# Four transposes in each feed-forward of a diffusion-transformer step: between two blocks of products instead of inside one

## The chip, the core and the metric

The kernel runs on one core of one Trainium2 chip. The metric is the device time of one launch in microseconds (us). Times of instructions below are in us, or in nanoseconds (ns) where marked so.

## What is computed

The reference is one inference step of a two-layer backbone. 128 context tokens and 128 latent tokens pass through the same weights, so every product has 256 columns of tokens. A layer is a mixer (latent and grouped-query attention in layer 0, differential attention in layer 1) and then a gated feed-forward. Each of these has a shift, a scale and a gate, six vectors of 2048 values per layer that come from a condition through `w_ada`.

```
mod = silu(cond) @ w_ada[l] + b_ada[l]             # sh1, sc1, gt1, sh2, sc2, gt2
h = rmsnorm(x, g_norm_mix[l]) * (1 + sc1) + sh1
x = x + gt1 * mixer(h)
h = rmsnorm(x, g_norm_ffn[l]) * (1 + sc2) + sh2
u = h @ w_up                                       # 2048 -> 2 * 5632
u = conv3(u) + b_conv                              # over positions, each feature by itself
x = x + gt2 * ((silu(gate) * val) @ w_down)        # 5632 -> 2048
```

## The kernel before

**Products.** Everything is float32. Each operand is split into a rounded high part and the remainder: a weight chunk becomes `wh` (by ScalarE, L237) and `wl` (by VectorE, L238), an activation becomes a high half and a low half of `hx`. `gemm` (L323) adds up one chunk of 128 output features in one PSUM bank `acc`. A block is 128 rows of the contraction, and it takes three products: `wh` by the high half, `wh` by the low half, `wl` by the high half. In the trace and in the order these read wh, wh, wl. A chunk of the up-projection has 16 blocks, 48 products, and a chunk of the down-projection has 22 blocks, 66 products. Every product is a load of 128x128 weights (PEld in the profile) and a matmul with 256 columns. 1024 columns, 8 blocks, make one tile of `wh` or `wl`, so that block 8 of an up chunk is the first of its second tile.

**The feed-forward.** `ffn` (L1246) runs once per layer. It takes half of the 88 chunks of `w_up`, two for each of the 22 features of a half, then the down-projection's 16 chunks over that half, and then both again (`NQ` is 2). The first three chunks arrive already multiplied (`ready`), since `modulated` (L666) starts them before the norm is known. The others go through `product`, which calls `gemm`.

**Sums of `w_ada`.** The vectors of `mod` are computed in units of 512 values. A unit's sums stand in a PSUM bank with the features along the free axis; ScalarE copies them to the tile `am`, TensorE transposes `am` in four pieces of 128x128 into the PSUM bank `misc` (`turn` in `ada_finish`, L411, with ident from the constants `cst`), and VectorE reduces these to `mod` (L424) and adds the bias (L426). One such unit, the first quarter of the feed-forward's gate, begins in `modulated`; its last step, the four transposes, is handed to `ffn` as the list `turn`.

**Order of the work.** A scheduler orders each engine's instructions, except those that `keep_order` has pinned. `ffn` pins the order of the first products that it computes itself: the list `in_order` holds what goes with each of them, nothing with two, `turn` with the third, nothing with the fourth. A callable `between` is called by `gemm` in block 8 behind the first of the block's three products (L334 to L336), so that the transposes stand between the two products that use the same `wh`. All three product kinds of these chunks and the transposes are pinned in this order.

Of the kernel before, what the change touches and what calls it, by code (L numbers as in the profile page):

```python
# [21 lines left out]
NT = 2 * T  # L22
# [66 lines left out]
def step_kernel(ctx: ExitStack, tc: tile.TileContext, A: dict):  # L89
# [4 lines left out]
    def keep_order(i):  # L94
        if not any(i is j for j in kept):
            kept[:] = [i]
            tc.keep_in_program_order(i)
# [28 lines left out]
    def banks(name):  # L126
        return tc.tile_pool(name=name, bufs=1, space=PSUM)
# [7 lines left out]
    def T_(pl, shape, tag, dt=F32, bufs=None):  # L135
        kw = {} if bufs is None else {"bufs": bufs}
        return pl.tile(shape, dt, tag=tag, name=nm(tag), **kw)
# [98 lines left out]
    def split(out_hi, out_lo, src, pin=lambda i: i):  # L236
        pin(act.copy(out_hi, src))  # L237
        pin(dve.tensor_tensor(out=out_lo, in0=src, in1=out_hi.bitcast(F32), op=ALU.subtract))  # L238
# [81 lines left out]
            pin(pe.matmul(ps[c][:, :NT], wl, xh(k), start=False, stop=b))  # L320
        return [p[:, :NT] for p in ps]

    def gemm(blocks, xh, xl, n=NT, first=0, between=None):  # L323

        fixed = lambda i: keep_order(i) if between is not None else i
        ps = T_(pacc, [P, 512], "acc")
        last = len(blocks) - 1
        for i in range(last + 1):  # L330
            k = (i + first) % (last + 1)
            wh, wl = blocks[k]
            fixed(pe.matmul(ps[:, :n], wh, xh(k), start=(i == 0), stop=False))
            if callable(between):  # L334
                if i == (last + 1) // 2:
                    between()  # L336
            elif between and i in between:
                between[i]()
            fixed(pe.matmul(ps[:, :n], wh, xl(k), start=False, stop=False))
            fixed(pe.matmul(ps[:, :n], wl, xh(k), start=False, stop=(i == last)))  # L340
        return ps[:, :n]


# [94 lines left out]
    def load_row():  # L438
        feat["row"] = T_(feat["home"], [P, 2, D], "condb")
        sp.dma_start(out=feat["row"], in_=A["condb"])  # L440
        for r in range(2):
            keep_order(act.activation(feat["row"][:, r], feat["row"][:, r], AF.Silu))
# [118 lines left out]
    def pump(rows, feats=0.0, until=None):  # L561

        until = until or RLIMIT[stage[0]]
        step()
        side_pump()
        ada["due"] += rows
        while ada["due"] >= 0.25:
            if ada["i"] >= until and not later:
                ada["due"] = 0.0
                break  # L570
            ada["due"] -= 0.25 if ada["i"] >= until else 0.25 * ada["pew"]
            row_step(until)
        feat["due"] += feats
        while feat["due"] >= 1.0 and feat["i"] < FLIMIT[stage[0]]:
            feat["due"] -= 1.0
            feature_step()
# [44 lines left out]
    def raw_rows(u, l, which):  # L621

        at = [0]

        def row(c):
            for g in range(2):
                s = slice(g * T, (g + 1) * T)
                act.activation(u[:, c, s], x[:, c, s], AF.Identity, scale=scl[:, l, which, c, g:g + 1])  # L630
            for g in range(2):
                s = slice(g * T, (g + 1) * T)
                dve.scalar_tensor_tensor(out=u[:, c, UW + g * T:UW + (g + 1) * T], in0=x[:, c, s],
                                         scalar=scl[:, l, which, c, g:g + 1],
                                         in1=u[:, c, s].bitcast(F32), op0=ALU.mult, op1=ALU.subtract)

        def behind(c):
            for _ in range(2 if c < KD - 1 else KD):
                if at[0] > c:
                    break  # L640
                if c == KD - 1:
                    ensure(l, 3 * which + 1)
                elif (l, 3 * which + 1, at[0] // 4) not in done:
                    break
                row(at[0])
                at[0] += 1

        return behind
# [14 lines left out]
    def raw_tile(pl, tag):  # L663
        return home(pl, tag)[:, :KD * 2 * UW].rearrange("p (k n) -> p k n", k=KD)
# [580 lines left out]

    def ffn(hx, W, ready, turn, l, st):  # L1246
        xh, xl = (lambda k: hx[:, k, :NT]), (lambda k: hx[:, k, NT:2 * NT])
        product = lambda: ready.pop(0) if ready else gemm(W.chunk(), xh, xl, between=in_order.pop(0) if in_order else None)
        WD = Weights(A["w_down"][l], KQ, TB)
        cw = ada["cw"]  # L1250
        with tc.tile_pool(name=f"ffn{l}", bufs=1) as fp, banks(f"pffn{l}") as pf:
            feat["home"], feat["pool"] = fp, pf
            feat["due"] = 0.0
            in_order = [{}, {}] + turn + [{}]
            T_(fp, [P, SHIFT // 4], "pad")

            def conv(m):
                early = bool(ready)
                pin = keep_order if early else lambda i: i
                ps = product()  # L1260
                y = T_(fp, [P, NT], "cv", bufs=3)
                pin(act.activation(y, ps, AF.Identity, scale=cw[:, 1, m:m + 1], bias=cw[:, 3, m:m + 1]))  # L1262
                y3 = y.rearrange("p (g t) -> p g t", g=2)
                p3 = ps.rearrange("p (g t) -> p g t", g=2)
                pin(dve.scalar_tensor_tensor(out=y3[:, :, 1:], in0=p3[:, :, :T - 1],  # L1265
                                             scalar=cw[:, 0, m:m + 1], in1=y3[:, :, 1:],
                                             op0=ALU.mult, op1=ALU.add))
                pin(dve.scalar_tensor_tensor(out=y3[:, :, :T - 1], in0=p3[:, :, 1:],  # L1268
                                             scalar=cw[:, 2, m:m + 1], in1=y3[:, :, :T - 1],
                                             op0=ALU.mult, op1=ALU.add))  # L1270
                if early and ready:
                    W.ahead(pin)
                return y

            def up(q):
                gs = []
                for i in range(q * KQ, (q + 1) * KQ):
                    rate = 0 if i < LATE else FRATE["up"]
                    fine[0] = False
                    gate = conv(i)  # L1280
                    pump(0, rate)
                    val = conv(NFF + i)
                    pump(0, rate)
                    act.activation(gate, gate, AF.Silu)
                    dve.tensor_tensor(out=val, in0=gate, in1=val, op=ALU.mult)
                    g = T_(fp, [P, ROW], "g", F32R, bufs=KQ)
                    split(g[:, :NT], g[:, NT:2 * NT], val)
                    gs.append(g)
                    if i == LATE - 1:
                        load_row()  # L1290
                return gs

            def down(gs, q):
                u, rows = None, None
                if q == NQ - 1 and l < NL - 1:
                    u = raw_tile(keep, "hx")
                    rows = raw_rows(u, l + 1, 0)
                for c in range(KD):
                    quiet = q == NQ - 1 and c >= KD - QUIET[0]
                    fine[0] = quiet  # L1300
                    if q == 0:
                        ensure(l, 5, [c // 4])
                    ps = gemm(WD.chunk(), lambda k: gs[k][:, :NT], lambda k: gs[k][:, NT:2 * NT])
                    if l == NL - 1 and q == NQ - 1 and c == KD - 1:
                        last_residual(ps, l, 1, c, st)
                    else:
                        residual(ps, l, 1, c, st if q == NQ - 1 else None)
                    if rows:
                        rows(c)
                    if l == NL - 1 and q == NQ - 1 and c in EARLY:  # L1310
                        act.activation(x[:, c], x[:, c], AF.Identity, scale=C("gfin")[:, c:c + 1])
                    pump(0, 0 if quiet else FRATE["down"])
                return u

            for q in range(NQ):
                gs = up(q)
                u = down(gs, q)
            while feat["i"] < FLIMIT[stage[0]]:
                feature_step()
            return u  # L1320


    with banks("pab") as ppool["ada"]:
# [3 lines left out]
        first = {1: load_half(1, 0, "araw"), 0: load_half(0, 0, "raw")}  # L1327
# [8 lines left out]
        with tc.tile_pool(name="beside", bufs=1) as beside:  # L1336
            o = mixer_ab(hx, rb0, beside)
            with tc.tile_pool(name="raw", bufs=1) as rp:
# [3 lines left out]
                W = Weights(A["w_up"][0], KD, 1)  # L1342
# [5 lines left out]
    with tc.tile_pool(name="cc", bufs=1) as cp, banks("pc") as ppool["ada"]:  # L1348
# [3 lines left out]
        W = Weights(A["w_in_c"], KD, 1)  # L1352
# [5 lines left out]
        W = Weights(A["w_up"][1], KD, 1)  # L1358
# [149 lines left out]
```

## Time and profile before

| | |
|---|---|
| time, median of 3 runs | 2363.69 us (2362.99 to 2365.67) |
| the profiled execution's own time | 2362.23 us |
| its span, first to last instruction | 2360.4 us |
| TensorE busy, and loading weights | 98% and 94% of the span |
| VectorE, ScalarE, GpSimdE busy | 78%, 50%, 7% |
| mean granted TensorE clock | 0.995 |
| read from HBM | 605.12 MB, 258 GB/s over the span |

The profile gives each engine's busy time, the span in 40 slices, and the chain of work that ended last. A busy TensorE says only that matmuls are in flight: the ends of its matmuls are modelled. How fast it works is read from the number of matmuls in a stretch of time, or from the length of an uninterrupted piece of the chain and its count.

### The profile page before, as it was taken

The numbers are of one execution on the slowest core, as the hardware profiler recorded it, in microseconds if no ns is written. First come the engines' busy times: TensorE is split into PE (matmuls) and PEld (weight loads), VectorE is DVE, ScalarE is ACT, GpSimd is POOL, SyncE is SP. The second block draws the span as 40 slices with busy tenths as digits, with TensorE's granted clock in tenths as the row PEclk, the third lists the DMA queues.
The fourth block names the chain that finished last, engine by engine and source line by source line (L and its number), as shares of the span: only waits on it lengthen the run. The fifth ranks groups of instructions, "written<-read, shape, count | busy, mean of one in ns | idle before, by whom it ended". The sixth has DMA issues, their size and how long they took to land.

```text
span 2360.4 us, 47894 instructions
## 1 busy us (share of the span) xinstructions
PE 2323.6 (98%) x19666; PEld 2214.8 (94%) x19666; DVE 1850.4 (78%) x2864; ACT 1191.4 (50%) x1980; POOL 176.7 (7%) x242
## 2 busy tenths in 40 slices
PE   6999999999999999999999999999999999999998
PEld 4788778999999999999999999999999999999998
DVE  3569767889989999999988888787998655666644
ACT  4246545665554455555564545557555434555443
POOL 0002101300000000001130000122000000000011
PEclk9999999999999999999999999999999999999999
DMA  9988888677777777677778888667666555555553
GB/s 362 352 327 300 305 321 325 239 281 265 267 259 283 295 271 267 251 263 273 281 279 304 302 293 315 233 249 274 251 250 242 183 193 181 193 181 190 185 185 119
DMA packets 106811, 612.97 MB, mean 260 GB/s; under 512 B 11552, under 2 KB 19552, under 8 KB 38880
## 3 DMA queue, kind: packets, MB, share of 16 engines
q1 hardware_dynamic: 106592, 609.92, 70.8%
q8 instruction: 154, 2.52, 0.4%
q14 instruction: 65, 0.53, 0.1%
HBM read 605.12 MB, written 4.75 MB: 258 GB/s over the span
## 4 chain that ended last, share of the span: by engine, by line
PE 96%; DVE 2%; DMA 1%; ACT 1%; issue 0%; SPq 0%; POOL 0%; DVEq 0%; ACTq 0%
PE acc L104 88%; PE ada L104 4%; PE att L104 2%; PE att L107 1%; PE misc L104 1%; DVE wl L238 1%; DMA araw<-w_ada 0%; PE ada L107 0%; ACT wh L237 0%; DMA raw<-w_in_ab 0%; DVE x L1370 0%; DVE aacc L481 0%; DVE nt L604 0%; DMA block<-w_ada 0%; DVE proj L960 0%
## 5 line engine op out<-in xcount | busy, mean ns | idle before, releaser
L104 PE MATMUL acc<-hx,wh 128*128 128x256 f32 (+1 forms) x7296 | 1280.3, 280 | 5.5 <-ACT hx L614 4.3
L237 ACT CAST wh<-raw 128x1024 fp32r<-128x1024 f32 (+2 forms) x824 | 794.5, 976 | 955.8 <-PE acc L104 760.1
L238 DVE TENSOR_TENSOR wl<-raw,wh 128x1024 fp32r<-128x1024 f32 (+2 forms) x824 | 920.2, 1132 | 309.6 <-ACT wh L237 307.0
L104 PEld LDWEIGHTS acc<-hx,wh 128*128 128x128 f32 x7296 | 1114.0, 189 | 37.9 <-issue 17.2
L104 PE MATMUL acc<-hx,wl 128*128 128x256 f32 (+1 forms) x3648 | 1016.7, 279 | 4.4 <-DVE wl L238 4.4
L104 PEld LDWEIGHTS acc<-hx,wl 128*128 128x128 f32 x3648 | 686.9, 188 | 5.5 <-DVE wl L238 5.5
L104 PE MATMUL acc<-g,wh 128*128 128x256 f32 x2816 | 488.2, 278 | 0.0
L104 PEld LDWEIGHTS acc<-g,wh 128*128 128x128 f32 x2816 | 429.2, 189 | 0.0
L104 PE MATMUL acc<-g,wl 128*128 128x256 f32 x1408 | 391.7, 278 | 0.0
L104 PE MATMUL acc<-hxc,wh 128*128 128x256 f32 (+1 forms) x1536 | 276.6, 281 | 0.0
L452 DVE CUSTOM_DVE_ANT_0 junk<-araw,condb 128x2048 f32<-128x2048 f32 x120 | 275.8, 2299 | 0.0
L104 PEld LDWEIGHTS acc<-g,wl 128*128 128x128 f32 x1408 | 264.2, 188 | 0.0
L104 PEld LDWEIGHTS acc<-hxc,wh 128*128 128x128 f32 x1536 | 235.9, 188 | 8.7 <-issue 8.4
L104 PE MATMUL acc<-hxc,wl 128*128 128x256 f32 (+1 forms) x768 | 213.5, 278 | 0.0
L200 POOL TENSOR_TENSOR sqacc<-sqacc,sq 128x256 f32<-128x256 f32 x62 | 71.1, 1146 | 1539.9 <-ACT sq L196 1533.3
L481 DVE SCALAR_TENSOR_TENSOR aacc<-block,condw,aacc 128x512 f32<-128x512 f32 x240 | 172.1, 755 | 12.4 <-DMA block<-w_ada 12.3
L104 PEld LDWEIGHTS acc<-hxc,wl 128*128 128x128 f32 x768 | 144.5, 188 | 0.3
L104 PE MATMUL ada<-araw,condw 128*32 128x512 f32 (+1 forms) x736 | 91.3, 591 | 12.8 <-DMA araw<-w_ada 12.8
L1262 ACT ACTIVATE cv<-acc,convw 128x256 f32<-128x256 f32 x170 | 95.0, 559 | 0.0
L773 DVE SCALAR_TENSOR_TENSOR x<-acc,mod,x 128x128 f32<-128x128 f32 x190 | 57.4, 344 | 39.7 <-PE acc L104 39.6
L1268 DVE SCALAR_TENSOR_TENSOR cv<-acc,convw,cv 128x254 f32<-128x254 f32 x170 | 81.4, 479 | 3.3
L1265 DVE SCALAR_TENSOR_TENSOR cv<-acc,convw,cv 128x254 f32<-128x254 f32 x170 | 80.8, 475 | 0.0
(229 smaller groups left out, 1400.4 us busy)
## 6 DMA issues: line engine op xcount, KB each, us to landing
raw<-w_up SPq DMA_DIRECT2D x176, 1024.0 KB, 4.8
araw<-w_ada SPq DMA_DIRECT2D x146, 1024.0 KB, 6.0
raw<-w_down SPq DMA_DIRECT2D x88, 1024.0 KB, 4.8
raw<-w_in_c SPq DMA_DIRECT2D x48, 1024.0 KB, 6.9
block<-w_ada SPq DMA_DIRECT2D x128, 256.0 KB, 5.4
raw<-w_in_ab SPq DMA_DIRECT2D x19, 1024.0 KB, 7.1
raw<-w_out_ab SPq DMA_DIRECT2D x16, 1024.0 KB, 7.0
raw<-w_out_c SPq DMA_DIRECT2D x16, 1024.0 KB, 5.8
```

The source lines that it names most:

```text
L104: return self.placed(nc.tensor.matmul(*a, **kw))
L107: return self.placed(nc.tensor.transpose(*a, **kw))
L200: eng.tensor_tensor(out=st["acc"], in0=st["acc"], in1=sq, op=ALU.add)
L237: pin(act.copy(out_hi, src))
L238: pin(dve.tensor_tensor(out=out_lo, in0=src, in1=out_hi.bitcast(F32), op=ALU.subtract))
L452: keep_order(dve.tensor_tensor_reduce(out=T_(feat["pool"], [P, D], "junk"), in1=feat["row"][:, c], in0=feat["raw"].rearrange("p g n -> p ( ...
L481: i = dve.scalar_tensor_tensor(out=acc[c], in0=block, scalar=condw[:, k, c:c + 1], in1=acc[c], op0=ALU.mult, op1=ALU.add)
L773: dve.scalar_tensor_tensor(out=x[:, c, s], in0=ps[:, s], scalar=mod[:, l, 3 * which + 2, c, g:g + 1], in1=x[:, c, s], op0=ALU.mult, op1=AL ...
L1262: pin(act.activation(y, ps, AF.Identity, scale=cw[:, 1, m:m + 1], bias=cw[:, 3, m:m + 1]))
L1265: pin(dve.scalar_tensor_tensor(out=y3[:, :, 1:], in0=p3[:, :, :T - 1], scalar=cw[:, 0, m:m + 1], in1=y3[:, :, 1:], op0=ALU.mult, op1=ALU.add))
L1268: pin(dve.scalar_tensor_tensor(out=y3[:, :, :T - 1], in0=p3[:, :, 1:], scalar=cw[:, 2, m:m + 1], in1=y3[:, :, :T - 1], op0=ALU.mult, op1=A ...
```

## The change

`gemm` gets a second hook, `behind`, which is called in the same block 8, but after the block's third product. `ffn` hands the unit's transposes to it in place of `between`. The chunks that are pinned are the same as before.

```
-    def gemm(blocks, xh, xl, n=NT, first=0, between=None):
+    def gemm(blocks, xh, xl, n=NT, first=0, between=None, behind=None):
...
-        fixed = lambda i: keep_order(i) if between is not None else i
+        fixed = lambda i: keep_order(i) if between is not None or behind else i
...
             fixed(pe.matmul(ps[:, :n], wh, xl(k), start=False, stop=False))
             fixed(pe.matmul(ps[:, :n], wl, xh(k), start=False, stop=(i == last)))
+            if behind and i == (last + 1) // 2:
+                behind()
         return ps[:, :n]
...
-        product = lambda: ready.pop(0) if ready else gemm(W.chunk(), xh, xl, between=in_order.pop(0) if in_order else None)
+        product = lambda: ready.pop(0) if ready else gemm(W.chunk(), xh, xl, **(in_order.pop(0) if in_order else {}))
...
-            in_order = [{}, {}] + turn + [{}]
+            in_order = [dict(between={})] * 2 + [dict(behind=t) for t in turn] + [dict(between={})]
```

What this does to the order of TensorE's instructions in layer 0's feed-forward, third chunk of those that it computes itself (`acc_5782` is the chunk's bank, `wh_5778` and `wl_5779` the weight tiles of blocks 8 to 15, `am_5605` the unit's sums; a line with - stands in the kernel before, one with + in the changed one):

```order
 L104 MATMUL acc_5782<-hx_5443,wh_5774 128x256 x2
 L104 MATMUL acc_5782<-hx_5443,wl_5775 128x256
-L104 MATMUL acc_5782<-hx_5443,wh_5778 128x256
-L107 MATMUL misc_5808<-cst_74,am_5605 128x128 x4
-L104 MATMUL acc_5782<-hx_5443,wh_5778 128x256
+L104 MATMUL acc_5782<-hx_5443,wh_5778 128x256 x2
 L104 MATMUL acc_5782<-hx_5443,wl_5779 128x256
+L107 MATMUL misc_5810<-cst_74,am_5605 128x128 x4
 L104 MATMUL acc_5782<-hx_5443,wh_5778 128x256 x2
 L104 MATMUL acc_5782<-hx_5443,wl_5779 128x256
```

The four transposes moved two products later, from between the two products with the same `wh` to between the `wl` product of block 8 and the first `wh` product of block 9. The same in layer 1's feed-forward:

```order
 L104 MATMUL acc_20251<-hx_19913,wh_20243 128x256 x2
 L104 MATMUL acc_20251<-hx_19913,wl_20244 128x256
-L104 MATMUL acc_20251<-hx_19913,wh_20247 128x256
-L107 MATMUL misc_20277<-cst_74,am_20075 128x128 x4
-L104 MATMUL acc_20251<-hx_19913,wh_20247 128x256
+L104 MATMUL acc_20251<-hx_19913,wh_20247 128x256 x2
 L104 MATMUL acc_20251<-hx_19913,wl_20248 128x256
+L107 MATMUL misc_20279<-cst_74,am_20075 128x128 x4
 L104 MATMUL acc_20251<-hx_19913,wh_20247 128x256 x2
 L104 MATMUL acc_20251<-hx_19913,wl_20248 128x256
```

The same move happened there. VectorE, ScalarE, GpSimdE and the DMA queue keep their instructions in the same order, and TensorE has no other place that differs; only line numbers behind `gemm` are two higher.

## The prediction

> **What bounds the kernel now.** I read the page first.
>
> ```profile
> PE 2323.6 (98%) x19666; PEld 2214.8 (94%) x19666; DVE 1850.4 (78%) x2864; ACT 1191.4 (50%) x1980; POOL 176.7 (7%) x242
> ...
> PE 96%; DVE 2%; DMA 1%; ACT 1%; issue 0%; SPq 0%; POOL 0%; DVEq 0%; ACTq 0%
> ```
>
> TensorE (PE) is busy for 98% of the span and makes up 96% of the chain that ended last. So an edit pays only if it changes the number of TensorE's instructions, a wait of TensorE, or the pace at which it takes its instructions. The number is the same here. Next I read the chain in order of time, at the two places where the edited transposes stand (misc, L107).
>
> ```profile
> 487.59 0.44 PE misc L107 x4
> 488.02 690.34 PE acc L104 x6090
> ...
> 1632.12 0.43 PE misc L107 x4
> 1632.56 715.04 PE acc L104 x6071
> ```
>
> Behind each of them there is a single piece of chain with no wait inside it: nearly all of the feed-forward of that layer. The first needs 690.34 / 6090 = 113.36 ns per product, the second 715.04 / 6071 = 117.78 ns. The products have the same shape and the same code. The difference is 4.42 ns per product, and over 6071 products it is 26.9 us, 1.1% of the kernel. That is the only thing at these places that is large, so I looked for what it hangs on, with the stages' table.
>
> ```profile
> core 0: us, PE busy (x) PEld busy (x) DVE busy (x) ACT busy (x) POOL busy (x), PEclk, DMA share, GB/s
> 500.00:1170.00 670.00, 670.00 (x5914) 670.00 (x5913) 624.61 (x802) 340.00 (x468) 16.40 (x13) 1.00 0.73 269
> 1640.00:2340.00 700.00, 700.00 (x5945) 700.00 (x5945) 470.19 (x618) 334.77 (x443) 15.77 (x13) 1.00 0.56 199
> ```
>
> The slower stage is layer 1 (700 / 5945 = 117.7 ns against 670 / 5914 = 113.3). It isn't slower by the clock: the granted clock (PEclk) is 1.00 in both. It isn't slower by load elsewhere: there VectorE (470 of 700 us), the DMA share (0.56) and the traffic (199 GB/s) are all lower than in layer 0. So TensorE has two rhythms for the same stream, and keeps the one it has fallen into for 6000 products. The question is what it falls into behind the transposes. The timeline of TensorE around them, first in layer 0, then the end of the same piece in layer 1:
>
> ```profile
> 487.31 0.28 PE L104 MATMUL acc<-hx,wh 128*128 128x256 f32 x1
> 487.42 0.60 PE L107 MATMUL misc<-cst,am 128*128 128x128 f32 x4
> 487.78 0.36 PE L104 MATMUL acc<-hx,wh 128*128 128x256 f32 x1
> 487.98 0.28 PE L104 MATMUL acc<-hx,wl 128*128 128x256 f32 x1
> 488.10 0.40 PE L104 MATMUL acc<-hx,wh 128*128 128x256 f32 x2
> 488.34 0.28 PE L104 MATMUL acc<-hx,wl 128*128 128x256 f32 x1
> 488.46 0.39 PE L104 MATMUL acc<-hx,wh 128*128 128x256 f32 x2
> ...
> 1632.63 0.40 PE L104 MATMUL acc<-hx,wh 128*128 128x256 f32 x2
> 1632.87 0.28 PE L104 MATMUL acc<-hx,wl 128*128 128x256 f32 x1
> 1632.99 0.40 PE L104 MATMUL acc<-hx,wh 128*128 128x256 f32 x2
> ```
>
> From one wl to the next is 0.36 us at 487.98, while a block in the fast rhythm takes 3 x 113.3 = 340 ns. So behind the transposes layer 0 too starts slowly, and is back to 0.39 for a pair of wh at 488.46; in layer 1 the pair stays at 0.40. The choice falls within the first two or three blocks behind the break, and no one asks again until the mixer or the end.
>
> **The change part by part.**
>
> *The break itself.* In layer 0 it is the time from 487.31 to 488.10, 0.79 us for three products and four transposes. Three products alone are 0.34 us, so the break costs 0.45 us. The nearest break of the new kind, four transposes of a unit's `am` behind a wl and ahead of a wh, stands in the mixer of layer 0:
>
> ```profile
> 416.80 0.28 PE L104 MATMUL acc<-hx,wl 128*128 128x256 f32 x1
> 416.92 0.60 PE L107 MATMUL ada<-cst,am 128*128 128x128 f32 x4
> 417.27 0.48 PE L104 MATMUL acc<-hx,wh 128*128 128x256 f32 x2
> 417.60 0.28 PE L104 MATMUL acc<-hx,wl 128*128 128x256 f32 x1
> 417.71 0.39 PE L104 MATMUL acc<-hx,wh 128*128 128x256 f32 x2
> ```
>
> From 416.80 to 417.71 is 0.91 us for four products (0.453 alone) and the transposes: 0.46 us. The change of the break's own cost is +0.01 us, and the rows' rounding puts it between -0.02 and +0.03. Twice that is nothing.
>
> *The transposes come 0.23 us later* (two products). The reader of `misc` is VectorE's reduction:
>
> ```profile
> 489.39 0.19 DVE L424 TENSOR_REDUCE mod<-misc 128x8 f32<-128x32 f32 x1
> ...
> 1633.92 0.18 DVE L424 TENSOR_REDUCE mod<-misc 128x8 f32<-128x32 f32 x1
> ```
>
> It starts 1.37 us behind the end of the transposes in the chain (488.02) and 1.37 behind 1632.55, held by VectorE's earlier work. So 0.23 us is hidden, with 1.1 us to spare; without that cover it would cost VectorE 0.23 us, and TensorE nothing as long as its weights are ahead. No other engine's order, no wait and no DMA moves, as the order shows. The wait for `wl` of block 8 now ends before the transposes instead of behind them. That takes away 0.45 us of cover from it, but TensorE showed no gap there.
>
> *The rhythm behind the break.* This is the term that matters. The trace before has breaks of both kinds, and the chain shows the pace of what follows each. First those where a unit's transposes of `am` stand between two blocks, the new place; the first, one near the middle, and the last:
>
> ```profile
> 37.76 0.22 PE ada L107 x2
> 37.98 7.07 PE acc L104 x60
> ...
> 417.08 0.44 PE ada L107 x4
> 417.52 21.77 PE acc L104 x192
> ...
> 1545.26 0.44 PE ada L107 x4
> 1545.70 32.66 PE acc L104 x288
> ```
>
> 32.66 / 288 = 113.4 ns and 21.77 / 192 = 113.4 are fast; 7.07 / 60 = 117.8 is slow. From the first to the last of these there are eight with 18 products or more behind them: the first, with two transposes, is slow, the other seven, with four, are fast. Now the old place, inside a block. There are five in which the unit's transposes come last, from 488.02 (fast) to 1632.56 (slow), and the three between these are like the first of them:
>
> ```profile
> 1219.91 0.44 PE ada L107 x4
> 1220.34 11.31 PE acc L104 x96
> ```
>
> 11.31 / 96 = 117.8 ns. So four of five were slow inside a block, and one of eight between blocks. The feed-forward of layer 0 is the lucky one of the five. Other short work doesn't keep to that, in either place:
>
> ```profile
> 220.19 0.44 PE misc L104 x4
> 220.64 2.12 PE acc L104 x18
> ...
> 1259.29 0.44 PE att L107 x4
> 1259.73 10.90 PE acc L104 x96
> ```
>
> The first four are spreads of a norm's factor between two blocks, and slow (2.12 / 18 = 117.8); the second four are transposes of another tile inside a block, and fast (10.90 / 96 = 113.5). So the place alone doesn't settle it.
>
> I take it that layer 1 goes to the fast rhythm and layer 0 stays in it. Layer 1 then gains 6071 x 4.42 ns = 26.9 us, layer 0 nothing. The bounds of this term are -26.9 us (layer 1 becomes fast) and +26.9 us (layer 0 becomes slow: 6090 x 4.42). I take the first, since it is nearest to the seven breaks that share the operation, the count and the place. Whether faster products then meet a wait is answered by layer 0: it ran at 113.36 ns without one, with VectorE at 624.61 of 670 us and 269 GB/s, more than layer 1 will ask for.
>
> [...]
>
> *The mixer of layer 1* lies between the two feed-forwards, from 1178 to 1632 us, with many breaks of its own. Its instructions and order are the same. All of it from one rhythm to the other would be 454 x 4.42 / 117.78 = 17 us, but each break chooses anew, so I allow ±2 us and take 0.
>
> *Sum.* Against the profiled execution: 2362.23 - 26.9 = 2335.3 us. It was 1.5 us below the median of the runs, 2363.69, from which the same sum gives 2336.8. I forecast 2336.0.
>
> **The rivals.**
>
> *Layer 1 falls into the slow rhythm again.* For it: the three blocks ahead of the break are the same, and the spreads of a norm between blocks were slow. Against it: seven of eight. Price 0: 2362.2 by the profile, 2363.7 by the median. [...]
>
> *The two layers change places*, layer 0 slow and layer 1 fast: -26.9 + 26.9, again about 2363. Layer 0's one break inside a block was fast, so its redraw can lose.
>
> *Slower: layer 0 loses the fast rhythm, and layer 1 doesn't find it.* The place is the piece from 488.02 on. The price is 6090 x 4.42 = 26.9 us: 2389 by the profile, 2390.6 by the median. It decides if the pair of wh at the third block behind the break still shows 0.40 instead of 0.39 us. For it: layer 0's present state is the exception among the five, so a new draw has something to lose there, and the first break between blocks was slow. Against it: it needs two slow outcomes where seven of eight were fast.
>
> That the change does not do what it says is excluded by the order, which shows the move in both layers.
>
> **How the numbers follow.** Seven of eight for each layer would give 0.77 for both fast. Three of these seven are followed by at most 24 products, and the slow spreads share the place, so I take less: 0.70 for the forecast, 0.18 for layer 1 slow again, 0.04 for the exchange, 0.08 for slower. The likeliest case's own range is 2332 to 2340: the two sums, ±2 for the mixer, and about ±2 for the spread of runs (2362.99 to 2365.67). It holds only 0.70, so the range must take in the two cases without a change, up to 2366: 2332 to 2366, which leaves out 0.08. A measurement of this kernel can tell about 0.2% (4.7 us) from no change. Faster 0.70, same 0.18 + 0.04 = 0.22, slower 0.08.
>
> **What would show it.** In the chain of the changed kernel the piece behind layer 1's transposes has 6069 products: 688 us confirms the forecast, 715 refutes it. The piece behind layer 0's has 6088: 690 us confirms, 717 refutes. The time per product should be 113.4 ns in both at a granted clock of 1.00, with no wait of TensorE between. The break should cost 0.45 us as before, and the reduction at L424 should start no later relative to the end of the transposes. I am wrong if the time falls with a pace that hasn't changed, or if the pace changes in the middle of a piece, without a break.

## The result, and the profile after

| | median, us | runs | ratio to the kernel before (95% interval) |
|---|---|---|---|
| before | 2363.49 (2362.08 to 2367.36) | 12 | |
| changed | 2364.68 (2357.75 to 2369.18) | 12 | 1.0002 (0.9991 to 1.0012) |

The change made no difference that can be measured. The forecast of 2336.0 us was wrong; the rival in which layer 1 falls into the slow rhythm again came true. The profiled execution took 2364.03 us, with a span of 2362.2.

The chain of waits of the changed kernel, at the transposes of layer 0 and of layer 1 (start, length, what, number of instructions):

```profile
487.97 0.44 PE misc L107 x4
488.41 690.11 PE acc L104 x6088
...
1633.65 0.43 PE misc L107 x4
1634.08 714.81 PE acc L104 x6069
```

The pieces have the 6088 and 6069 products that the move implies, and their paces are those of before: 690.11 / 6088 = 113.36 ns and 714.81 / 6069 = 117.78 ns. The stages' table has the same numbers of matmuls as before, 5914 and 5945, at a clock of 1.00:

```profile
500.00:1170.00 670.00, 670.00 (x5914) 670.00 (x5914) 624.38 (x802) 340.24 (x468) 16.44 (x13) 1.00 0.73 269
1640.00:2340.00 700.00, 700.00 (x5945) 700.00 (x5945) 470.84 (x618) 335.15 (x444) 15.71 (x13) 1.00 0.56 199
```

The timeline around layer 1's transposes shows the break in its new place:

```profile
1633.37 0.28 PE L104 MATMUL acc<-hx,wl 128*128 128x256 f32 x1
1633.49 0.60 PE L107 MATMUL misc<-cst,am 128*128 128x128 f32 x4
1633.84 0.48 PE L104 MATMUL acc<-hx,wh 128*128 128x256 f32 x2
1634.16 0.28 PE L104 MATMUL acc<-hx,wl 128*128 128x256 f32 x1
1634.28 0.40 PE L104 MATMUL acc<-hx,wh 128*128 128x256 f32 x2
```

From 1633.37 to 1634.28 it is 0.91 us for four products and the transposes, as forecast. Little was lost elsewhere. The mixer of layer 1 took 1.1 us longer, inside the 2 us that the prediction allowed: TensorE waited there for a transfer of `w_ada` in the middle of a unit's sums, and the 129 products behind these, from 1198.59 us on, ran at 117.7 ns by their starts, where the kernel before ran them at 113.3. The expected gain simply never began.

The starts in the trace are kept to 1 ns, though the rows round them to 10. "By the starts" below means by these unrounded ones. By them the first transpose begins 115 ns behind the last product's start in layer 0 and 119 ns in layer 1, in the kernel before and in the changed one; this distance is called the first gap. So the two streams arrive at the transposes in different states, though both at 113.3 ns a product, and the change left both states as they were. The first gap became the lead for the experiments.

### The profile page after: what moved, and what is told of

The parts are those of the page before. It is cut to its first block, busy times and chain, and to the rows that moved or that the text cites. A ratio compares the mean times of both kernels' runs of the same rounds, so it can differ in the third digit from the quotient of the medians.

```text
span 2362.2 us, 47894 instructions
## 1 busy us (share of the span) xinstructions
PE 2322.5 (98%) x19666; PEld 2213.5 (94%) x19666; DVE 1850.1 (78%) x2864; ACT 1191.6 (50%) x1980; POOL 177.0 (7%) x242
## 4 chain that ended last, share of the span: by engine, by line
PE 95%; DVE 2%; DMA 2%; ACT 0%; issue 0%; POOL 0%; DVEq 0%; SPq 0%; ACTq 0%
PE acc L104 87%; PE ada L104 4%; PE att L104 2%; DMA araw<-w_ada 1%; PE att L107 1%; PE misc L104 1%; DVE wl L238 1%; DMA raw<-w_in_ab 0%; PE ada L107 0%; DMA x<-xT 0%; DVE sqacc L200 0%; DVE aacc L483 0%; DVE x L1372 0%; ACT wh L237 0%; DVE nt L606 0%
```

## The experiments

Theory A: the pace behind a break is fixed by the state in which the stream arrives and by the number of transposes, and the place has no part in it. Theory B, that of the prediction: the place loads a draw. Theory C: layer 1's stream is slow by itself.

Each kernel was compared with the kernel before in runs on the same chip. There it took 2365.03 us (median of 13 runs), 2364.02 (13) and 2365.01 (7) in the three sittings.

### One transpose more, in layer 1

```
-            for b in range(2 if on_dve else 4):
+            for b in [0, 1, 2, 3, 3] if l and pin is keep_order else range(2 if on_dve else 4):
```

> A fifth transpose (the fourth once more, to the same place) stands behind the four in layer 1, and nothing else differs from the changed kernel. Theory A, what follows a break is fixed by the state in which the stream arrives and by the instructions of the break, not by its place: the break is 0.11 us longer, so its outcome may change: about 2364 us + 0.1 if layer 1 stays at 117.8 ns a product, 2337 us if it goes to 113.4. Theory B, the place decides by a loaded draw: fast in most cases, 2337 us. Theory C, layer 1's stream settles at 117.8 ns by itself, whatever the break: 2364 us, and no break can change it.

Measured: 2336.8 us, ratio 0.9875 (0.9856 to 0.9893). The chain of this kernel at layer 1:

```profile
1636.83 0.55 PE misc L107 x5
1637.38 687.86 PE acc L104 x6069
```

687.86 / 6069 = 113.34 ns. A redundant instruction of 0.11 us saved 28 us, about the 26.9 that the prediction had priced. Theory C falls, and so does any doubt about the price. VectorE and the DMA kept up, as layer 0 had suggested.

### The same four in the first chunk, in both layers

```
-            in_order = [dict(between={})] * 2 + [dict(behind=t) for t in turn] + [dict(between={})]
+            in_order = [dict(behind=t) for t in turn] + [dict(between={})] * 3
```

> The same four transposes, behind block 8 of the first chunk that the feed-forward computes itself in place of the third, in both layers: 96 products earlier in the same stream. Theory A: the stream arrives in the same state, so layer 0 stays fast, layer 1 slow, 2364 us. Theory B: a new draw, 2337 us in most cases. Theory C: 2364 us.

Measured: 2364.4 us, ratio 0.9988 (0.9963 to 1.0014). Nine of ten runs lay between 2363.0 and 2368.3 us, and one, the profiled one, took 2336.55. In that one the chain shows layer 1 fast:

```profile
1618.42 4.33 PE acc L104 x35
1622.75 0.44 PE misc L107 x4
...
1623.19 698.74 PE acc L104 x6165
```

698.74 / 6165 = 113.34 ns. Here only 35 products lie between the last sums of the unit and the transposes, where the changed kernel has 131, and by the starts this stream arrived slow. So near another break the arriving state can differ from run to run. The nine others have no trace; that they arrived fast is inferred from their times. The run doesn't tell A from B by itself.

### Many breaks

Every third chunk of the up-projection got a break (transposes between products) of 1, 2, 3, 4, 5, 6, 8 and again 1, 2, ... transposes of `am`, 27 in each layer. In the first kernel they lie between two blocks in layer 0 and inside a block in layer 1; in the second the places are exchanged (`l == 0`).

```
+    def more(n):
+        pt = bank()
+        for b in range(n):
+            keep_order(pe.transpose(pt[:, b % 4 * P:(b % 4 + 1) * P], last_am[0][:, b % 4 * P:(b % 4 + 1) * P], ident))
...
+            for n in (1, 2, 3, 4, 5, 6, 8) * 4:
+                in_order += [dict(between={})] * 2 + [dict(extra=(l == 1, n))]
```

> Beside the unit's transposes, every third chunk of the up-projection gets a break of 1, 2, 3, 4, 5, 6 or 8 further transposes of the same tile into the free bank, whose results nobody reads: between two blocks in layer 0, inside a block (behind its first product) in layer 1; about 26 breaks in each layer, 110 transposes, 13 us of TensorE in each. Theory A: the pace behind a break goes with the number of transposes and with the pace ahead of it, and the same pair gives the same pace each time. Theory B: most pieces are fast in layer 0 and slow in layer 1, whatever the number. Theory C: pieces in layer 1 go to 117.8 ns whatever the break, those in layer 0 to 113.4. Time: 2390 us plus or minus 30.

> As the run before, with the two places exchanged: inside a block in layer 0, between two blocks in layer 1. Theory A: the same number of transposes gives the same pace as there for the same pace ahead, in either layer and place. Theory B: pieces mostly slow in layer 0, mostly fast in layer 1. Theory C: as in the run before, layer 1 slow and layer 0 fast. Time: 2390 us plus or minus 30.

Measured: 2375.6 and 2382.0 us, one run each. The chain of the first kernel in layer 1, with the added breaks inside a block:

```profile
1675.21 0.11 PE misc L107
1675.32 16.97 PE acc L104 x144
1692.29 0.22 PE misc L107 x2
1692.51 16.35 PE acc L104 x144
1708.86 0.33 PE misc L107 x3
1709.19 16.96 PE acc L104 x144
1726.15 0.44 PE misc L107 x4
1726.59 16.34 PE acc L104 x144
```

And of the second, at the same breaks, now between two blocks:

```profile
1681.73 0.11 PE misc L107
1681.84 16.96 PE acc L104 x144
1698.81 0.22 PE misc L107 x2
1699.03 16.35 PE acc L104 x144
1715.38 0.33 PE misc L107 x3
1715.70 16.96 PE acc L104 x144
1732.67 0.44 PE misc L107 x4
1733.10 16.34 PE acc L104 x144
```

144 products take 16.96 us slow (117.8 ns) and 16.34 us fast (113.5). The two columns agree line by line. With the unit's own there are 56 breaks in each kernel, and at all 56 the pace ahead and the pace behind are the same in both, though 54 of them had exchanged their places. Theory B falls: the place has no part in these outcomes. From the ninth added break in layer 0, and from the first in layer 1, both run through one cycle: 1 leaves a slow stream slow, 2 frees it, 3 make it slow, 4 free it, 5 and 6 keep it fast, 8 make it slow. Among these breaks, four on a slow stream left it fast 14 times out of 14. Four on a fast stream left it fast 4 times (layer 0, first gap 115 ns) and slow twice (layer 1, 119 ns).

### Five, in the kernel before

The same edit as in the first experiment, on the kernel before, whose transposes stand inside the block.

> The kernel before, with the fifth transpose in layer 1 alone; all transposes stay inside the block, behind its first product. Theory A (arriving state and number of transposes decide, the place doesn't): layer 1 goes to 113.4 ns a product as it did with five between blocks, 2336.8 us, 27 below the kernel before. Theory B (the place decides, the fifth only made a new draw): inside a block it is slow in most cases, 2364 us.

Measured: 2338.1 us, ratio 0.9890 (0.9875 to 0.9904); the piece of the chain behind the transposes in layer 1:

```profile
1635.23 688.09 PE acc L104 x6071
```

That is 113.34 ns a product. In layer 1, inside or between, five leave the stream fast and four leave it slow. The place is out.

### One transpose ahead, in layer 1

```
-            in_order = [dict(between={})] * 2 + [dict(behind=t) for t in turn] + [dict(between={})]
+            in_order = [dict(between={}), dict(behind=one) if l else dict(between={})] + [dict(behind=t) for t in turn] + [dict(between={})]
```

> The changed kernel, and in layer 1 a single further transpose (its result is not read) behind block 8 of the chunk ahead, 48 products before the four, which stay as they are. Theory A: in the runs with many breaks one transpose on a stream that arrives like layer 1's (first gap 119 ns) left it fast but in the other state, in which the next break begins with 115 ns, and four on that state stayed fast each time. So the same four now leave layer 1 fast: 2337 us. Theory B: the four are the same in the same place and leave layer 1 slow: 2364 us.

Here `one` is a single transpose of `am` whose result nobody reads.

Measured: 2365.5 us, ratio 1.0004 (0.9993 to 1.0015).

```profile
1626.14 0.11 PE misc L107
1626.25 5.46 PE acc L104 x48
1631.71 0.44 PE misc L107 x4
...
1632.15 714.81 PE acc L104 x6069
```

The single left the stream fast (5.46 us for 48), as forecast, but the four behind it began with a gap of 120 ns, not 115, and made it slow. Four on a fast stream with a gap of 119 or 120 were slow here too; what failed is my rule for how a stream comes into that state.

### Three and one

No instruction is added; the fourth transpose and the reduction that reads them move to block 8 of the next chunk.

```
+            parted = l == 0 and pin is keep_order
+            for b in range(2 if on_dve else 3 if parted else 4):
...
+                if parted:
+                    pin(pe.transpose(pt[:, 3 * P:], got["am"][:, 3 * P:], ident))
...
+            in_order = [dict(between={})] * 2 + [dict(behind=t) for t in turn] + [dict(behind=lambda: rest.pop()()) if l == 0 else dict(between={})]
```

> The changed kernel, but in layer 0 three of the four transposes stand behind block 8 and the fourth behind block 8 of the next chunk; no instruction is added. Theory A: three on a stream that arrives in layer 0's state (first gap 115 ns) left it slow each time, and one on a slow stream left it slow each time, so layer 0 goes to 117.8 ns a product, 27 us more: 2391 us. Theory B: two draws between blocks, fast in most cases: 2364 us. If the four together were merely lucky, both are open.

Measured: 2391.3 us, ratio 1.0112 (1.0097 to 1.0127). The chain in layer 0:

```profile
492.38 0.33 PE misc L107 x3
492.70 5.66 PE acc L104 x48
498.36 0.11 PE misc L107
...
498.47 711.42 PE acc L104 x6040
```

711.42 / 6040 = 117.8 ns: layer 0 is slow, as the outcomes of the many breaks had it, and the price is the 27 us named for the slower rival. In layer 1 (`l == 1`):

> The same parting in layer 1, with layer 0 as in the changed kernel; no instruction is added. Theory A: three on layer 1's arriving state (fast, first gap 119 ns) has not been seen, so it has no forecast: 2337 us if it is left fast and the one behind it keeps it so, 2364 us if three leave it slow, since one on a slow stream leaves it slow. Either way the single transpose must do what it did before on the state it meets.

Measured: 2339.0 us, ratio 0.9891 (0.9876 to 0.9906).

```profile
1636.25 0.33 PE misc L107 x3
1636.58 5.66 PE acc L104 x48
1642.23 0.11 PE misc L107
...
1642.34 682.41 PE acc L104 x6021
```

Three make it slow, and here the single frees it: 682.41 / 6021 = 113.3 ns. "One leaves a slow stream slow" was too simple. By the starts the single begins 124 ns behind the last product here, and 121 ns in layer 0.

### Where the single stands

The slow pieces of these two kernels differ in their weight loads (product, number, busy us, mean ns of one); first between the two breaks of layer 0, then of layer 1:

```profile
L104 PEld LDWEIGHTS acc<-hx,wh 128*128 128x128 f32 x26 | 4.0, 190 | 0.0
L104 PEld LDWEIGHTS acc<-hx,wl 128*128 128x128 f32 x13 | 2.4, 188 | 0.0
```

```profile
L104 PEld LDWEIGHTS acc<-hx,wh 128*128 128x128 f32 x23 | 3.5, 188 | 0.0
L104 PEld LDWEIGHTS acc<-hx,wl 128*128 128x128 f32 x12 | 2.3, 192 | 0.0
```

One load in three is longer, a wh (half of them, so that their mean is 190) in layer 0, and the wl in layer 1. I took its distance from the break for the missing part of the state and moved the single within its block. Of the lines below, the first is from the kernel with layer 0 parted, the others are from the one with layer 1 parted; `...` stands for what is as before.

```
+            in_order = ... + [dict(between=lambda: rest.pop()()) if l == 0 else dict(between={})]
...
+            if second and i == (last + 1) // 2:
+                second()
+            in_order = ... + [dict(second=lambda: rest.pop()()) if l == 1 else dict(between={})]
```

> As three and one in layer 0, but the single transpose stands inside its block, behind the block's first product, instead of behind its third. Theory A, refined: a slow stream carries one longer weight load (192 ns, the others 188) in each group of three products, and what a break does to it depends on how far back that load lies. With the single behind the third product the longer load was third from last, and the stream stayed slow; here it is the last ahead of the break, as it was in layer 1, where the single made the stream fast. So the second break frees layer 0: 2364 us, with 48 slow products between the two breaks. Theory A without this refinement (the place never matters): layer 0 stays slow, 2391 us. Theory B (inside is mostly slow): 2391 us.

> As three and one in layer 1, but the single transpose stands behind the second product of its block instead of behind the third. Theory A, refined: the longer load is then the third from last ahead of the break, as in layer 0 with the single behind the block, so the stream stays slow: 2364 us. Without the refinement: fast behind the single as before, 2339 us.

Measured: 2392.0 us (ratio 1.0113, 1.0092 to 1.0133) and 2335.9 us (0.9869, 0.9847 to 0.9891). Both times the outcome stayed as it was with the single behind the block, against the refinement. So theory A holds in its plain form: the place doesn't matter on a slow stream either, and the distance of the longer load isn't the state. The first gap, 121 and 124 ns, was also unchanged by the move.

## Why the prediction was wrong

**The bound, the two paces and their price held.** Making layer 1 fast saved 28 us in the first experiment and 25 to 29 in the three others that did so; making layer 0 slow cost 27 both times. The term was 26.9. In the kernel before the two pieces hold the same 6071 products of 256 columns; layer 0's has 19 more at its end, from 1175.93 us on, which have 258 columns and are the next mixer's. Without them it ran at 113.35 ns, so the price stands.

**The break's own cost and the hidden delay held.** The break took 0.91 us for four products and the transposes, and the reduction, at 1635.24, came 1.16 us behind their end in the chain (1634.08), inside the cover that was named.

**The step that failed is the rhythm behind the break**: "four of five were slow inside a block, and one of eight between blocks", read as an effect of the place. The runs showed that the place has none: with the places of 54 breaks exchanged every outcome stayed, and in layer 1 four transposes left 117.8 ns a product and five 113.3, inside a block and between blocks. What goes with the outcome is the number of transposes together with the state in which the stream arrives. Three things were mixed in the count. First, the number of transposes. I grouped by "the unit's transposes come last", but at 1219.91 the unit's four follow four others. The chain of the kernel before:

```profile
1219.47 0.44 PE att L107 x4
1219.91 0.44 PE ada L107 x4
...
1352.26 0.33 PE att L107 x3
1352.59 0.44 PE ada L107 x4
```

Of the four breaks inside a block that left 117.8 ns a product, three had eight or seven transposes, not four. Second, the state on arrival. Of the seven breaks between blocks that left 113.4 ns, four were met, by the starts, at 117.8 ns a product, and in the runs with many breaks four transposes of `am` freed a slow stream every time. Third, so the comparison left only one case like layer 1's, four transposes of `am` on a fast stream with a first gap of 119 ns, and that was layer 1 itself, slow. In the seven traces that have the case there, with 119 or 120 ns (both kernels, the two with many breaks, one ahead, and three and one in layer 0 with either place of the single) it was slow each time.

**The first rival's condition was the right one**: "the three blocks ahead of the break are the same". Moving the break by two products of an unbroken stream left what arrives as it was: the first gaps are 115 and 119 ns in both kernels. The rival was given 0.18, though the one case that matched layer 1's break, four on a first gap of 119 ns, was that break itself in the kernel before, and slow.

**What stays open.** What the state is, and what sets it. For the transposes of `am` in the two feed-forwards the first gap goes with the outcome for a given number, in all the traces. It isn't the whole state: in the mixer of layer 1 four transposes of another tile (`dev`, at 1380.95 us in the kernel before) met a fast stream with a first gap of 119 ns too, and left it fast. Nor do the order and the rows show where 115, 119 or 124 ns come from: the single ahead (120 instead of 115) and the longer load were both misses. The transposes of a break follow each other every 109 ns, so its number and its length grew together in every run; which of the two counts was not told apart.

## What to carry to other kernels

When a saturated TensorE runs two stretches of the same products at different paces with the clock fully granted, count the matmuls per time first: the pace can be set by the last short interruption and last for hundreds of microseconds, as it did here. Try a change of what the interruption contains before one of where it stands, and read the pace of the piece behind it from a trace. In layer 1 one transpose more, or a break parted in two, took 25 to 29 us (1.1 to 1.3%) off this kernel, where moving it took nothing; the same parting in layer 0 cost 27 us, so what helps depends on the stream that it meets. Before counting cases of an effect, group them by everything that differs, above all by the state ahead and the number of instructions, or a pattern of thirteen cases shows what isn't there.

## What was not expected of the hardware

The same stream of weight loads and 256-column matmuls runs at 113.3 or at 117.8 ns a product, and in each piece of about 6000 of them it held its pace to the end in every trace. Breaks switched it, and short waits did too: at 174.59 us of the kernel before, a product that starts 0.1 us late between others has 113.3 ns a product ahead of it and 117.8 behind. In the feed-forwards the response to breaks was reproducible, 56 of 56 in two kernels. Behind a unit's sums it was not: the 129 products behind those at the start of layer 1's mixer ran at 113.3 ns in the kernel before and at 117.7 in the same kernel with a fifth transpose, which comes only later. In the slow pace one weight load in three is recorded with 192 ns in place of 188. A longer break can be the cheaper one: in layer 1 five transposes were 26 and 28 us better than four.
